# A decoder layer on one core: gate and query projections with the tokens stationary, rotary tables on GpSimd, another opening

## The chip, the cores and the metric

The kernel runs on one core of a Trainium2 chip. A core has five engines that run their own instruction streams and meet through semaphores: TensorE (PE in the profile; its weight loads are PEld), VectorE (DVE), ScalarE (ACT), GpSimd (POOL) and SyncE (SP), which here issues every DMA. The metric is the device time of one execution in microseconds. The kernel before takes 640.01 us (median of three runs, 639.51 to 640.58).

## The reference, cut to what matters

One layer of a hybrid decoder: 256 tokens, width 1024, everything in float32.

```python
xn = rmsnorm(h, norm_mix_g)                                  # per token: x * rsqrt(mean(x^2)+EPS) * g
q_a, k_a, v_a, q_b, f_b, i_b, og_b, g_a, g_b = split_cols(xn @ w_in)   # nine projections of 1024 columns
y_a = moba_attention(q_a, k_a, v_a, positions) @ w_br_attn   # 16 heads of 64, rotary on q and k
y_b = hgrn2(q_b, f_b, i_b, og_b, lb, hgrn_norm_g) @ w_br_hgrn          # 8 heads of 128
merged = sigmoid(g_a) * y_a + sigmoid(g_b) * y_b
h = h + merged @ w_out
h = h + memory_cross_attention(...)                          # 4 heads of 256, 256 memory tokens
h = h + (silu(gate) * up) @ w_ffn_out                        # hidden width 2816
out = rmsnorm(h, final_norm_g)

# hgrn2, with lb from a softmax over learned logits
q = silu(q_b) * 128 ** -0.5
f = lb + (1 - lb) * sigmoid(f_b)                             # forget gate
k = 1 - f
S_t = diag(f_t) S_{t-1} + k_t i_t^T ;   o_t = S_t^T q_t
o = rmsnorm_per_head(o) * norm_g * silu(og_b)

# rotary: cos and sin of position * 10000^(-2i/64), i = 0..31
```

## The kernel before, in words

**Weights as 103 chunks.** All weight matrices are cut on the host into chunks of 128x2048 (1 MB each), in the order in which TensorE uses them (`plan`, `ORDER`). To keep float32 accuracy each chunk is split on the chip: `prep` issues the DMA into `raw` (two buffers), ScalarE writes `hi`, the value rounded to fp32r, in two pieces of 1024 columns, and `lo = raw - hi` is made by VectorE (576 columns of each piece) and GpSimd (448 columns, `POOL_COLS` is 896 for a chunk). `hi` and `lo` have three buffers each. A product is three matmuls: hi·hi, hi·lo and lo·hi. `nxt` hands the next chunk to TensorE and prepares the one two ahead (`LEAD`).

**Two forms of product.** In the F form (`f_part`, `gemm_f`) a chunk holds 256 columns and all 1024 rows of the weight; the weight is the stationary operand, the 256 tokens move, and the result has features on partitions: 48 matmuls of 128x256 a chunk. In the T form (`t_part`, `gemm_t`) a chunk holds 512 columns and half of the rows; 128 tokens are stationary, 512 weight columns move, and the result has tokens on partitions: 24 matmuls of 128x512 a chunk, and two chunks make one group of 512 columns for the 256 tokens.

**Order of the work.** TensorE's instructions stand in the order in which the Python code records them; those of ScalarE, VectorE, GpSimd and SyncE are put into an order of their own by a scheduler at build time. Once that order is fixed, each engine runs its list strictly in order: an instruction that waits holds back all that stand behind it. A helper, `tick`, is called after each chunk and advances background work (`bg`) by one step, and `later` holds functions that run at the next tick.

The opening (`opening`, `prep(pieces=4)`) brings the input `xT` and the first two chunks in quarters of 256 KB each; the split input is `Xh`, `Xl`. TensorE first runs 18 matmuls on zeros (`warm`). Then come four F chunks of the forget gate (columns 4096 to 5119 of `w_in`, tiles `psg` and `psf`), whose eviction `ev_f` multiplies by the row factors `rows_x`, applies Sigmoid, and makes the gate `fT` and the keys `KS`; then four F chunks of the recurrence's queries (columns 3072 to 4095), whose eviction `ev_q` makes `QQ` and, on GpSimd, `QP`. The norm factor `r_x` comes from squares of `xraw` on ScalarE and VectorE and two small matmuls, and `rows_x` from two transposes of it. The rotary tables `Ct`, `St` (`rope_tables`, 42 small VectorE instructions and two Sin on ScalarE) are made meanwhile.

All that follows is in T form up to the cross attention: values of the recurrence (`Vb`), then values, queries and keys of the attention, output gate, the two merge gates, and so on. The recurrence itself (`hgrn`: 18 blocks of small matmuls, tiles `l`, `lp`, `lv`, with VectorE work between them) runs as background steps between the chunks, beginning behind the last query chunk. Then come cross attention and feed-forward, which the change does not touch.

Of the kernel before, what the change touches and what calls it, by code (L numbers as in the profile page):

```python
# [24 lines left out]
EPS = 1e-6  # L25
NEG = -1e30
LEAD = 2
POOL_COLS = 896
WARM = 18
# [11 lines left out]
def plan():  # L41
    order = []
    for name, base in (("f", 4), ("q", 3)):
        order += [("F", "w_in", base * 1024 + c * 256) for c in range(4)]
# [4 lines left out]
    for base in (5, 2, 0, 1, 6):  # L49
        order += tgroup("w_in", base * 1024)  # L50
# [61 lines left out]
def build(tc, A, out):  # L112
    nc = tc.nc
    V, SC, G, PE, SY = nc.vector, nc.scalar, nc.gpsimd, nc.tensor, nc.sync
    with ExitStack() as ctx:
# [36 lines left out]
        V.memset(ones, 1.0)  # L152

# [4 lines left out]
        def prep(tags=None, pieces=2, raw=None):  # L158
            i = made[0]
            made[0] += 1  # L160
            if raw is None:
                raw = wr.tile([128, 2048], F32, name="raw", tag="raw")
# [7 lines left out]
            if pieces == 2:  # L170
                SY.dma_start(raw, A["w"][i])
            for c in range(pieces):
                a = slice(c * n, (c + 1) * n)
                if pieces > 2:
                    SY.dma_start(raw[:, a], A["w"][i][:, a])
                    yield
                SC.activation(hi[:, a], raw[:, a], AF.Copy)  # L177
                cut = (c + 1) * n - POOL_COLS // pieces
                for eng, b in ((V, slice(c * n, cut)), (G, slice(cut, (c + 1) * n))):
                    eng.tensor_tensor(lo[:, b], raw[:, b], hi[:, b].bitcast(F32), op=ALU.subtract)  # L180
# [128 lines left out]
        opening = [prep(pieces=4), prep(pieces=4, raw=big("B14", "raw1", (128, 2048)))]  # L309
        for c in range(4):  # L310
            SY.dma_start(xraw[:, 2 * c:2 * c + 2], A["xT"][:, 2 * c:2 * c + 2])
            for g in opening:
                next(g)
            for k in (2 * c, 2 * c + 1):
                g1 = gv[:, V_MIX + k:V_MIX + k + 1]
                if k % 2 == 0:
                    SC.activation(Xh[:, k], xraw[:, k], AF.Copy, scale=g1)
                else:
                    V.tensor_scalar(Xh[:, k], xraw[:, k], g1, None, op0=ALU.mult)
                V.scalar_tensor_tensor(Xl[:, k], xraw[:, k], g1, Xh[:, k].bitcast(F32),  # L320
                                       op0=ALU.mult, op1=ALU.subtract)
        for g in opening:
            run(g)
# [19 lines left out]

        def ev_f(c):
            def ev(ps):
                for m in range(2):
                    h = 2 * c + m
                    t = t2("fraw", (128, 256))
# [760 lines left out]
```

## Time and profile before

| | |
|---|---|
| median of three runs | 640.01 us (639.51 to 640.58) |
| the profiled execution's own time | 641.26 us |
| its span, first to last instruction | 639.5 us |
| mean granted TensorE clock | 0.991 |
| instructions | 9044 |
| first matmul on weights | 7.39 us |
| start of the first `Vb` chunk | 66.98 us |

In the lines of the profile, `L177 ACT ... hi<-raw 128x1024` is a group of instructions of line 177 on ScalarE that write `hi` from `raw`; "x186" is how many, then come busy time in us and the mean of one in ns, and behind the bar the idle time of the engine before them with what ended it. A row of the timeline has start, duration, engine, line, operation and tiles, a count, and in brackets the idle time before it with what ended it. A row of the table by stage gives for a stretch of time the busy time of every engine, the granted TensorE clock as a share of full speed, the DMA engines' busy share and their rate. Matmuls are pipelined: a 128x512 matmul is listed with 390 ns, and the next one starts 227 ns after it. What TensorE needs for a block of work is therefore read from start to start.

### The profile page before, as it was taken

Reading aid. Unit: us, or ns where it says so; the run is one execution under the profiler, and the core shown is the slowest. Engines: PE = TensorE matmul, PEld = TensorE weight load, DVE = VectorE, ACT = ScalarE, POOL = GpSimd, SP = SyncE. Lnnn points to the kernel's source line nnn. Section 1 sums busy time; section 2 is a strip of 40 time slices with the busy share of each in tenths; the row PEclk is TensorE's granted clock in tenths of the full one; section 3 lists DMA queues with packets and bytes.
Section 4 is the critical chain, followed back from the end, with each engine's and each line's share of the span. In section 5 each row is a group of like instructions: output and inputs, shape, how many; then the busy total and the mean of one; then the engine's idle time right before and its main releaser. Section 6 shows DMA issues by size and latency. Waiting matters only on the chain.

```text
span 639.5 us, 9044 instructions
## 1 busy us (share of the span) xinstructions
PE 624.7 (98%) x3428; PEld 533.6 (83%) x3428; DVE 405.9 (63%) x713; ACT 321.5 (50%) x506; POOL 369.4 (58%) x258
## 2 busy tenths in 40 slices
PE   8989999999999999999999999999999999999995
PEld 7979888888887877778889999888888888888884
DVE  6996898789857777695556546764344444444433
ACT  5383564433368666673446445564444444444433
POOL 3468654376554664346766767656565555665552
PEclk9998999999999999999999999999999999999998
DMA  8634554444443333545545455462355554555511
GB/s 282 216 128 162 197 198 169 157 166 138 152 179 132 132 132 132 181 149 197 180 155 192 148 197 183 165 248 81 133 197 198 181 175 178 194 194 197 198 67 66
DMA packets 17036, 107.56 MB, mean 168 GB/s; under 512 B 2144, under 2 KB 2272, under 8 KB 4576
## 3 DMA queue, kind: packets, MB, share of 16 engines
q1 hardware_dynamic: 16992, 106.98, 47.2%
q8 instruction: 27, 0.44, 0.3%
q14 instruction: 17, 0.14, 0.1%
HBM read 105.92 MB, written 1.05 MB: 167 GB/s over the span
## 4 chain that ended last, share of the span: by engine, by line
PE 91%; DVE 3%; POOL 2%; issue 2%; DMA 1%; ACT 1%; SPq 0%; POOLq 0%; DVEq 0%
PE pst L220 13%; PE pst L222 13%; PE pst L221 13%; PE psi L222 6%; PE psi L220 6%; PE psi L221 6%; PE psf L217 3%; PE psf L216 3%; PE psf L215 3%; PE acc L222 3%; PE acc L220 3%; PE acc L221 3%; PE lp L524 2%; PE pso L220 1%; PE pso L222 1%
## 5 line engine op out<-in xcount | busy, mean ns | idle before, releaser
L180 POOL TENSOR_TENSOR lo<-raw,hi 128x448 fp32r<-128x448 f32 (+1 forms) x194 | 298.5, 1554 | 207.9 <-ACT hi L177 198.2
L177 ACT ACTIVATE hi<-raw 128x1024 fp32r<-128x1024 f32 (+1 forms) x194 | 195.6, 1036 | 189.6 <-PE pst L222 79.3
L180 DVE TENSOR_TENSOR lo<-raw,hi 128x576 fp32r<-128x576 f32 (+1 forms) x194 | 197.4, 1021 | 122.5 <-ACT hi L177 121.3
L220 PE MATMUL pst<-hi,Xh 128*128 128x512 f32 x224 | 90.5, 404 | 0.0
L222 PE MATMUL pst<-hi,Xl 128*128 128x512 f32 x224 | 87.4, 390 | 0.0
L221 PE MATMUL pst<-lo,Xh 128*128 128x512 f32 x224 | 87.3, 390 | 0.0
L220 PE MATMUL psi<-hi,h2h 128*128 128x512 f32 x176 | 69.6, 395 | 0.0
L222 PE MATMUL psi<-hi,h2l 128*128 128x512 f32 x176 | 68.6, 390 | 0.0
L221 PE MATMUL psi<-lo,h2h 128*128 128x512 f32 x176 | 68.5, 389 | 0.0
L222 PEld LDWEIGHTS pst<-hi,Xl 128*128 128x128 f32 x224 | 42.0, 188 | 9.0
L220 PEld LDWEIGHTS pst<-hi,Xh 128*128 128x128 f32 x224 | 42.1, 188 | 8.7 <-issue 0.7
L221 PEld LDWEIGHTS pst<-lo,Xh 128*128 128x128 f32 x224 | 42.1, 188 | 7.9
L222 PEld LDWEIGHTS psi<-hi,h2l 128*128 128x128 f32 x176 | 33.0, 188 | 7.1
L221 PEld LDWEIGHTS psi<-lo,h2h 128*128 128x128 f32 x176 | 33.1, 188 | 6.6
L220 PEld LDWEIGHTS psi<-hi,h2h 128*128 128x128 f32 x176 | 33.1, 188 | 6.5
L220 PE MATMUL acc<-hi,hid 128*128 128x512 f32 x88 | 34.3, 390 | 0.0
L222 PE MATMUL acc<-hi,hid 128*128 128x512 f32 x88 | 34.2, 389 | 0.0
L221 PE MATMUL acc<-lo,hid 128*128 128x512 f32 x88 | 34.2, 389 | 0.0
L217 PE MATMUL psf<-Xh,lo 128*128 128x256 f32 x96 | 29.3, 306 | 4.1 <-DVE lo L180 2.2
L215 PE MATMUL psf<-Xh,hi 128*128 128x256 f32 x96 | 28.6, 298 | 0.0
L216 PE MATMUL psf<-Xl,hi 128*128 128x256 f32 x96 | 28.3, 295 | 0.0
L1000 DVE SCALAR_TENSOR_TENSOR fu<-psi,r_h,fg 128x256 f32<-128x256 f32 x22 | 10.6, 484 | 26.0 <-ACT fg L998 25.8
(316 smaller groups left out, 1266.8 us busy)
## 6 DMA issues: line engine op xcount, KB each, us to landing
raw<-w SPq DMA_DIRECT2D x95, 1024.0 KB, 4.8
raw<-w SPq DMA_DIRECT2D x8, 256.0 KB, 5.6
xraw<-xT SPq DMA_DIRECT2D x4, 256.0 KB, 5.5
H<-xtok SPq DMA_DIRECT2D x1, 1024.0 KB, 8.7
mraw<-mT SPq DMA_DIRECT2D x1, 1024.0 KB, 5.6
out<-H SPq DMA_DIRECT2D x4, 256.0 KB, 2.2
gfin<-gfin SPq DMA_DIRECT2D x1, 512.0 KB, 6.5
cst<-cst SPq DMA_DIRECT2D x1, 272.0 KB, 5.7
```

The lines of the kernel that those rows point to most:

```text
L177: SC.activation(hi[:, a], raw[:, a], AF.Copy)
L180: eng.tensor_tensor(lo[:, b], raw[:, b], hi[:, b].bitcast(F32), op=ALU.subtract)
L215: PE.matmul(ps, lh, rh, start=first, stop=False)
L216: PE.matmul(ps, lh, rl, start=False, stop=False)
L217: PE.matmul(ps, ll, rh, start=False, stop=last)
L220: PE.matmul(ps, xh, h, start=first, stop=False)
L221: PE.matmul(ps, xh, l, start=False, stop=False)
L222: PE.matmul(ps, xl, h, start=False, stop=last)
L524: PE.matmul(ps[:, j], KS[:, a0 + j], QQ[:, a0 + j], start=True, stop=True)
L1000: V.scalar_tensor_tensor(u, ps[:, 256:512], r, g, op0=ALU.mult, op1=ALU.mult)
```

## The change

The change touches the opening, the gate and query projections, the rotary tables and a few steps that hang on them:

- The four F chunks of the gate and the four F chunks of the queries become four and four T chunks. The gate's come in the order: columns 0 to 511 rows 0 to 511, columns 512 to 1023 rows 0 to 511, then the other halves of the rows. The evictions work on tokens-on-partitions tiles: Tanh (gate) and Silu (queries) on ScalarE with the per-token factor as scale, straight from PSUM. The results are then turned by TensorE, 8 transposes of 128x128 for each half (`turned`, two ticks later), and `fT`, `KS`, `QP`, `QQ` are made from the turned tiles. `QP` is made on VectorE from PSUM, no longer on GpSimd, and `QQ` is copied by ScalarE.
- `r_x` comes from two ScalarE squares over the token-major input `H` (1024 columns, with an accumulator), so the load of `H` is recorded at the opening; `rows_x`, the squares of `xraw`, two small matmuls and two transposes go.
- The input comes in six transfers instead of four, the first two of 128 KB; the second chunk's quarters come behind all quarters of the first, and the second half of the input behind those.
- For the first eight chunks (`ALONE`) all of `lo` is made by VectorE.
- `rope_tables` runs on GpSimd: each multiply-add becomes two instructions, and an absolute value goes to ScalarE.
- The recurrence starts one tick later, and no drain stands before its output stage. The queries no longer carry a factor of two, hence 128 instead of 512 times EPS.
- A one-element Exp stands at ScalarE's head.

```diff
...
 LEAD = 2
 POOL_COLS = 896
+ALONE = range(8)
 WARM = 18
...
-    for name, base in (("f", 4), ("q", 3)):
-        order += [("F", "w_in", base * 1024 + c * 256) for c in range(4)]
...
+    order += [("T", "w_in", 4096 + c * 512, kh) for kh in range(2) for c in range(2)]
+    for base in (3, 5, 2, 0, 1, 6):
         order += tgroup("w_in", base * 1024)
...
+        warm_act = cp.tile([128, 1], F32, name="warm_act")
+        SC.activation(warm_act, ones, AF.Exp)
...
+            pieces = 4 if first else 2
             n = 2048 // pieces
...
-                cut = (c + 1) * n - POOL_COLS // pieces
+                cut = (c + 1) * n - (0 if i in ALONE else POOL_COLS // pieces)
                 for eng, b in ((V, slice(c * n, cut)), (G, slice(cut, (c + 1) * n))):
-                    eng.tensor_tensor(lo[:, b], raw[:, b], hi[:, b].bitcast(F32), op=ALU.subtract)
+                    if b.start < b.stop:
+                        eng.tensor_tensor(lo[:, b], raw[:, b], hi[:, b].bitcast(F32), op=ALU.subtract)
...
+        opening = [prep(), prep(raw=big("B14", "raw1", (128, 2048)))]
+
...
+        def take_x(a, b):
+            SY.dma_start(xraw[:, a:b], A["xT"][:, a:b])
+
+        for k in range(4):
+            if k in (0, 1, 2):
+                take_x(k, (1, 2, 4)[k])
+            next(opening[0])
+            part_x(k)
+        run(opening[0])
+        run(opening[1])
+        for k in (4, 6):
+            take_x(k, k + 2)
+        for k in range(4, 8):
+            part_x(k)
...
+        gate_a = cp.tile([128, 8], F32, name="gate_a")
+        gate_b = cp.tile([128, 8], F32, name="gate_b")
+        V.tensor_scalar(gate_a, oml, 0.5, None, op0=ALU.mult)
+        V.tensor_tensor(gate_b, lbt, gate_a, op=ALU.add)
...
+        def turned(th, c, use):
+            def turn():
+                for b in range(2):
+                    bk = bank("fT_", (128, 2, 256))
+                    for j in range(2):
+                        for t in range(2):
+                            PE.transpose(bk[:, j, t * 128:(t + 1) * 128],
+                                         th[t][:, (2 * b + j) * 128:(2 * b + j + 1) * 128], ident)
+                    use(4 * c + 2 * b, bk)
+            later.append(lambda: later.append(turn))
...
+            th = {}
+
+            def use(h0, bk):
+                for j in range(2):
+                    h = h0 + j
+                    dst = fT[:, 2 * h:2 * h + 2].rearrange("p a b -> p (a b)")
+                    if j == 0:
+                        SC.activation(dst, bk[:, j], AF.Identity, scale=gate_a[:, h:h + 1], bias=gate_b[:, h:h + 1])
+                    else:
+                        V.tensor_scalar(dst, bk[:, j], gate_a[:, h:h + 1], gate_b[:, h:h + 1],
+                                        op0=ALU.mult, op1=ALU.add)
+                a = slice(2 * h0, 2 * h0 + 4)
+                SC.activation(KS[:, a], fT[:, a], AF.Copy, scale=-1.0, bias=1.0)
+
+            def ev(t, ps):
+                th[t] = t2("fth")
+                SC.activation(th[t], ps, AF.Tanh, scale=r_half[:, t:t + 1])
+                if t == 1:
+                    turned(th, c, use)
...
+            def use(h0, bk):
+                a = slice(2 * h0, 2 * h0 + 4)
+                q4 = bk.rearrange(v4, a=2)
+                V.tensor_tensor(QP[:, a], q4, fT[:, a], op=ALU.mult)
+                SC.activation(QQ[:, a, 64:192], q4, AF.Copy)
                 odd = QP[:, a].rearrange("p a (b c) -> p a b c", c=2)[:, :, :, 1]
                 SC.activation(QQ[:, a, 0:64], odd, AF.Copy)
+
+            def ev(t, ps):
+                th[t] = t2("qth")
+                SC.activation(th[t], ps, AF.Silu, scale=r_x[:, t:t + 1])
+                if t == 1:
+                    turned(th, c, use)
...
-        pss = [[p.tile([128, 256], F32, name="psg", tag=n) for _ in range(2)]
-               for p, n in ((mm, "mm"), (sm, "sm"))]
+        run(prep())
+        run(prep())
         SY.dma_start(cst, A["cst"])
         run(prep())
+        SY.dma_start(H, A["xtok"])
         SY.dma_start(lm, A["lm"])
         SY.dma_start(posi, A["pos"])
...
-        for c in range(4):
-            square(xraw, c)
-        feature_sum(xraw)
-        w2 = by_k(nxt(1), 8)
...
-        r_x = feature_rstd(xraw, "x")
...
-        rows_x = rows_of(r_x, "x", "rowsA")
-        f_part(ps3[:, 1], w3, X, 1, range(7, 8))
-        for c, ps in enumerate(pss + [ps2, ps3]):
-            ev_f(c)(ps)
...
+        for t in range(2):
+            t_part(pss[0][t], w, X, t, 1)
+        ssqx = small("ssqx", [2])
+        junk = big("B9", "junk", (128, 2, 1024))
+        for t in range(2):
+            SC.activation(junk[:, t], H[:, t], AF.Square, accum_out=ssqx[:, t:t + 1])
+        r_x = rstd_of(ssqx, "x")
         r_half = cp.tile([128, 2], F32, name="r_half")
         V.tensor_scalar(r_half, r_x, 0.5, None, op0=ALU.mult)
+        ev = ev_f(0)
+        for t in range(2):
+            ev(t, pss[0][t])
+        tick()
+        w = by_k(nxt(), 4)
+        ev = ev_f(1)
+        for t in range(2):
+            t_part(pss[1][t], w, X, t, 1)
+            ev(t, pss[1][t])
+        tick()
...
-            V.tensor_copy(posf, posi)
...
             def rnd(o, src, c):
-                V.tensor_scalar(o, src, c, None, op0=ALU.mult)
-                V.tensor_scalar(o, o, RND, None, op0=ALU.add)
-                V.tensor_scalar(o, o, RND, None, op0=ALU.subtract)
+                G.tensor_scalar(o, src, c, None, op0=ALU.mult)
...
             def acc(o, a, c, b):
-                V.scalar_tensor_tensor(o, a, float(c), b, op0=ALU.mult, op1=ALU.add)
+                G.tensor_scalar(u, a, float(c), None, op0=ALU.mult)
+                G.tensor_tensor(o, u, b, op=ALU.add)
...
+            G.tensor_tensor(r, r, ml, op=ALU.add)
+            yield 1
+            G.tensor_scalar(r, r, lim, -lim, op0=ALU.min, op1=ALU.max)
+            yield 1
+            SC.activation(t, r, AF.Abs)
+            G.tensor_scalar(t, t, -1.0, TWO_PI / 4, op0=ALU.mult, op1=ALU.add)
+            yield 1
             SC.activation(m, r, AF.Sin)
             SC.activation(mh, t, AF.Sin)
             for i in range(2):
                 rs = r_x[:, i:i + 1]
...
-                    V.tensor_scalar(Ct[:, i, c * 32:(c + 1) * 32], mh[:, i], rs, None, op0=ALU.mult)
...
+                    G.tensor_scalar(Ct[:, i, c * 32:(c + 1) * 32], mh[:, i], rs, None, op0=ALU.mult)
...
-                    V.tensor_scalar(v, ssq, 1.0 / 128.0, 512.0 * EPS, op0=ALU.mult, op1=ALU.add)
+                    V.tensor_scalar(v, ssq, 1.0 / 128.0, 128.0 * EPS, op0=ALU.mult, op1=ALU.add)
...
+        start(rt)
+        for c in range(2):
+            gemm_t(X, ev_q(c))
         hg = hgrn()
-        for c in range(4):
-            if c == 2:
-                start(hg)
-            gemm_f(X, ev_q(c), bank("psf", (128, 2, 256)) if c == 0 else None)
-        start(rt)
+        next(hg)
+        start(hg)
...
-        drain(hg)
...
-        SY.dma_start(H, A["xtok"])
```

In the order that the scheduler gave the changed kernel, ScalarE's list reads, from the gate's last evictions on: the two ScalarE parts of the first turned gate half (`fT`), `hi` of the sixth chunk (two pieces), two `KS`, the absolute value of the rotary chain, a load of the Sin table, the first Sin, `hi` of the seventh chunk (two pieces), two `fT`, the second Sin, a load of the Silu table, the first query eviction, `hi` of the eighth chunk with two `KS` between, the second query eviction. GpSimd's list reads: `r_x`, then the rotary chain, with the six products `Tt` of the recurrence's first four heads among its last steps, then the tables, the other `Tt`, and from the ninth chunk on `lo`. TensorE's list reads: four gate chunks, 8 transposes, the first query chunk, 8 transposes, two query chunks, 8 transposes, the last query chunk, the first `Vb` chunk, 8 transposes, the recurrence's first block, the next `Vb` chunk. SyncE's list reads: input and first two chunks, third and fourth chunk, constants, `H`, fifth chunk, masks, positions, then the rest.

More of the change, by code (lines that the diff above doesn't have):

```diff
@@ L168, in prep @@
                 lo = big(tags[1], "lox", (128, 2048), F32R)
+            pieces = 4 if first else 2
             n = 2048 // pieces
-            if pieces == 2:
+            if not first:
                 SY.dma_start(raw, A["w"][i])
@@ L354, in ev_f @@
             return ev
         def ev_q(c):
[L357 to L366 removed]
+            th = {}
```

100 lines of the change are left out of this document (36 added, 64 removed).

## The prediction

> **What bounds the kernel now.** I read the page's shares first, then TensorE's waits, then the table by stage for the first 66 us.
>
> ```profile
> PE 624.7 (98%) x3428; PEld 533.6 (83%) x3428; DVE 405.9 (63%) x713; ACT 321.5 (50%) x506; POOL 369.4 (58%) x258
> PE 91%; DVE 3%; POOL 2%; issue 2%; DMA 1%; ACT 1%; SPq 0%; POOLq 0%; DVEq 0%
> ```
>
> TensorE is busy 624.7 of 639.5 us and carries 91% of the chain that ended last. What the change can win is TensorE's work, its waits, or its slow clock.
>
> ```profile
> PE psf L217 <- DVE lo L180: 2.2, 3, 0.9
> PE psf L217 <- POOL lo L180: 1.8, 1, 1.8
> PE psg L215 <- ACT hi L177: 1.6, 1, 1.6
> PE warm L308 <- DVE still L305: 1.6, 1, 1.6
> ```
>
> These are all waits of the whole span, and all lie in the gate and query stage: behind it TensorE is never idle.
>
> ```profile
> 0.00:7.40 7.40, 4.22 (x19) 3.92 (x19) 2.85 (x15) 2.67 (x5) 0.20 (x4) 1.00 0.62 161
> 7.40:13.40 6.00, 6.00 (x27) 5.84 (x27) 5.70 (x10) 4.75 (x9) 4.89 (x6) 1.00 1.02 372
> 13.40:21.80 8.40, 8.40 (x72) 8.40 (x72) 8.33 (x13) 4.61 (x7) 4.71 (x5) 1.00 0.84 301
> ...
> 41.00:47.00 6.00, 3.96 (x29) 3.35 (x27) 6.00 (x12) 5.75 (x10) 5.61 (x8) 1.00 0.24 100
> 47.00:53.00 6.00, 4.86 (x22) 4.86 (x23) 2.80 (x4) 0.15 (x1) 5.76 (x8) 0.54 0.53 175
> 53.00:59.00 6.00, 6.00 (x47) 6.00 (x47) 3.48 (x4) 3.84 (x6) 3.81 (x4) 0.89 0.45 178
> ```
>
> The third column from the right is the granted clock, the last the rate of the transfers in GB/s. At 41 to 47 us TensorE is busy 3.96 of 6.00 us, and behind that the clock is 0.54 and 0.89: 6 x 0.46 + 6 x 0.11 = 3.4 us of work lost. A long wait of TensorE costs itself and up to 3.4 us more. From 7.4 to 13.4 us TensorE does 27 matmuls and afterwards 72 in 8.4 us: the opening, too, runs at about half speed.
>
> **The change, part by part.**
>
> ```profile
> 7.39 0.58 PE L215 MATMUL psg<-Xh,hi 128*128 128x256 f32 x1 [1.61 <-ACT hi L177]
> 13.52 0.28 PE L215 MATMUL psg<-Xh,hi 128*128 128x256 f32 x1
> 17.82 0.28 PE L215 MATMUL psg<-Xh,hi 128*128 128x256 f32 x1
> ...
> 66.98 0.53 PE L220 MATMUL pst<-hi,Xh 128*128 128x512 f32 x1
> ...
> 79.36 1.46 PE L478 MATMUL l<-QQ,KS 128*128 128x192 f32 x8
> 80.52 0.53 PE L220 MATMUL pst<-hi,Xh 128*128 128x512 f32 x1
> 86.11 1.46 PE L478 MATMUL l<-QQ,KS 128*128 128x192 f32 x8
> ...
> 140.14 1.03 PE L656 MATMUL rT<-cst,ra 128*128 128x128 f32 x8
> 141.01 1.47 PE L524 MATMUL lp<-QQ,KS 128*128 128x192 f32 x8
> ```
>
> *TensorE's own work.* From 13.52 to 17.82 us lie 36 matmuls of 128x256: 0.119 us each, 5.73 us for an F chunk of 48. A T chunk of 24 takes 80.52 to 86.11 = 5.59 us. Eight chunks: 45.8 becomes 44.7 us, a gain of 1.1. Eight transposes take 140.14 to 141.01 = 0.87 us; 32 are added, 3.5 us, and six tiny instructions go (about 0.5). Net +1.9 us of work. Any gain must come from the waits and the clock.
>
> *Opening.*
>
> ```profile
> 4.83 0.51 ACT L317 ACTIVATE Xh<-xraw,gv 128x256 fp32r<-128x256 f32 x1 [1.65 <-DMA xraw<-xT]
> 6.71 1.30 ACT L177 ACTIVATE hi<-raw 128x512 fp32r<-128x512 f32 x2 [1.37 <-DMA raw<-w]
> ```
>
> The input's first 256 KB are there at 4.83, the first weight quarter at 6.71, and the first matmul stands behind them at 7.39. With 128 KB of input ahead of the quarter instead of 256, and no quarter of the second chunk beside it, I put its landing in the middle, 5.8, and the first matmul 0.9 us earlier: 6.5 us (between 5.5 and 7.4). Each quarter step of a gate chunk is now 6 matmuls of 128x512, 1.4 us at full clock, against 0.7 us for its 256 KB at 372 GB/s and 0.35 more for 128 KB of input in the first chunk: the transfers keep ahead. The clock stays slow for 6 us before; I take 5 us after, which costs 2.4. So TensorE is through four gate chunks at 6.5 + 4 x 5.45 + 2.4 = 30.7 (5.45 where chunk follows chunk, without the first matmul's longer step), through the first 8 transposes at 31.5, the first query chunk 37.1, 8 transposes 38.0, the second query chunk 43.6. There the seventh chunk is due. These times matter only as long as that chunk is ready; what follows says that it is not.
>
> *The rotary chain on GpSimd, and who queues behind it.* ScalarE's list has the absolute value of that chain, a Sin table load and the first Sin ahead of `hi` of the seventh chunk. ScalarE runs its list in order, so this chunk waits for GpSimd's chain, and TensorE for the chunk.
>
> ```profile
> L496 POOL TENSOR_TENSOR Tt<-fT 128x512 f32<-128x512 f32 x2 | 2.2, 1094 | 1.6 <-DVE fT L351 1.6
> L496 POOL TENSOR_TENSOR Tt<-Tt 128x64 f32<-128x64 f32 x2 | 0.6, 294 | 0.2
> L271 POOL TENSOR_TENSOR r_x<-v__359,nhalf 128x2 f32<-128x2 f32 x1 | 0.7, 707 | 4.2 <-DVE v__359 L269 4.2
> 50.77 1.38 POOL L496 TENSOR_TENSOR Tt<-Tt 128x128 f32<-128x128 f32 x4
> 48.05 1.21 POOL L496 TENSOR_TENSOR Tt<-Tt 128x256 f32<-128x256 f32 x1
> 48.04 0.74 DVE L180 TENSOR_TENSOR lo<-raw,hi 128x576 fp32r<-128x576 f32 x1
> L415 DVE TENSOR_SCALAR rt<-rt 128x64 f32<-128x64 f32 x3 | 0.6, 196 | 0.1
> L425 DVE TENSOR_TENSOR rt<-rt 128x64 f32<-128x64 f32 x1 | 0.2, 227 | 0.0
> L177 ACT ACTIVATE hi<-raw 128x1024 fp32r<-128x1024 f32 x186 | 191.0, 1054 | 188.2 <-PE pst L222 79.3 <-PE psi L222 35.5 <-PE acc L222 28.0
> L446 ACT ACT_TABLE_LOAD x1 | 1.3, 1283 | 0.0
> L832 ACT ACTIVATION_READ_ACCUMULATOR hjunk<-H 128x1 f32 x12 | 2.2, 187 | 0.0
> 33.69 0.26 ACT L446 ACTIVATE rt<-rt 128x64 f32<-128x64 f32 x1 [8.00 <-DVE rt L442]
> L361 ACT ACTIVATE qth<-qraw 128x512 f32<-128x512 f32 x4 | 2.5, 628 | 4.2 <-DVE qraw L360 4.2
> L353 ACT ACTIVATE KS<-fT 128x512 f32<-128x512 f32 x4 | 2.5, 624 | 0.4 <-DVE fT L351 0.3
> L279 ACT ACTIVATE rows_x<-rb 128x256 f32<-128x256 f32 x1 | 0.4, 363 | 0.0
> L360 DVE TENSOR_TENSOR qraw<-psf,rows_x 128x512 f32<-128x512 f32 x4 | 2.7, 680 | 4.7 <-PE psf L217 4.7
> ```
>
> The row of 33.69 shows the pattern already before: ScalarE sat 8.00 us behind VectorE's chain, and `hi` of a chunk stood behind it. The other rows are prices: two evictions and a `KS` (512 columns), a 256-column copy out of PSUM for `fT`, a product out of PSUM on VectorE. Now the new chain's end:
>
> 1. *Start.* `r_x` stands first on GpSimd and needs `H`, which lands behind 6.6 MB. By the table: 7.4 x 161 GB/s = 1.2 MB, 6 x 372 = 2.2, the other 3.2 at 372 to 301 take 8.7 to 10.7: 22.1 to 24.1, I take 23.1. Two squares at 1.05 + 0.19 = 2.5, `r_x` 0.71, a small VectorE step and handovers 0.4: 26.7 us. The fifth chunk, whose buffer is free when the third chunk's `lo` is done (near 20), the masks and the positions (1.3 MB, 3.5 us) are behind `H` on the queue and land by about then, so neither holds the chain up by itself.
> 2. *Length.* 43 instructions stand before the absolute value: 15 with two tensors and 28 with one. The nearest GpSimd row is the two-tensor 128x64 product, 0.294; VectorE takes 0.227 for such a one and 0.196 for a one-tensor one, so I scale: 0.294 x 0.196 / 0.227 = 0.25. Four dependent products take 1.38 us, some 0.08 between two. 15 x 0.37 + 28 x 0.33 = 14.8 us. The six `Tt` between add 1.09 + about 0.65 + 1.38 = 3.1.
> 3. *The shared port.* The 128x256 product at 48.05 took 1.21 us, where 0.65 fits between its neighbours: a VectorE `lo` ran from 48.04 to 48.78. Four `lo` pieces of 1024 columns (576 take 0.74, so 1.3 each) fall into the chain: 3.5 us (between 0 and 5.2).
>
> The chain ends at 26.7 + 14.8 + 3.1 + 3.5 = 48.1 us (bounds: VectorE's 0.196 for the one-tensor ones and no port loss, 43.0; 0.39 for them, twice VectorE, and full loss, 53.7). Then absolute value 0.26, table 1.28, Sin 0.26, first half of `hi` 1.05, its `lo` 1.3: 52.2, less one matmul that needs `hi` alone: 51.9. TensorE waits 51.9 - 43.6 = 8.3 us. The clock falls; of up to 3.4 us I take 2.5.
>
> *The rest of the stage.* Seventh chunk 51.9 + 5.45 + 2.5 = 59.9; transposes 60.7; eighth chunk 66.3. The transposes need both query evictions, which stand far down ScalarE's list: from 49.9 (first Sin done) two `hi` 2.1, two `fT` 0.7, Sin 0.26, table 1.28, eviction 0.63, `hi` 1.05, two `KS` 1.25, `hi` 1.05, eviction 0.63 make 58.9, so they add nothing; had the clock stayed up, they would be the next to be late, by 1.5 us. The first `Vb` chunk thus starts at 66.3 instead of 66.98, but 8 transposes (0.87) and the recurrence's first block (79.36 to 80.52, 1.16), done by then before, still follow: 66.3 + 2.0 = 68.3, that is +1.4 us.
>
> *At nothing.* `lo` on VectorE alone: 2.6 us a chunk against TensorE's 5.6; without that cover the chunk would be late by its excess. The one-element Exp: ScalarE loads a table at the head in both. Table loads before `Vb`: three in both. `H` on SyncE's list stands after two chunks and ahead of the fifth, due at 31.5, which lands near 26. `QP` moves to VectorE (four at 0.68 us), 2.7 us against the two multiplications per eviction that VectorE loses (0.68 and more, four times); it is one of the things that VectorE has room for while TensorE is late. The later tick and the missing drain: 18 blocks fit into the 20 ticks before the output stage.
>
> **Sum:** 640.0 + 1.4 = 641.4 us; against the profiled execution 641.3 + 1.4 = 642.7. The measurement tells about 0.2%, 1.3 us, from no change.
>
> A rule that speaks against this change: the Trainium skill, GPSIMD Engine Reference, section "Performance versus the Vector engine", calls ordinary elementwise work on GpSimd about twice VectorE's time. The rows here show 294 against 227 ns at this size, 1.3 times. By the page's factor on every instruction the chain would be some 6 us longer, an estimate, and the time about 648.
>
> **The rivals.**
>
> *Faster: the chain is shorter than I price it.* GpSimd's one-tensor instructions as short as VectorE's and no loss at the port: end at 43.0, 5.1 us earlier, 641.4 - 5.1 = 636.3. If the chain did not stand in front of the seventh chunk at all, that chunk would start at 43.6 and all follow 8.3 + 2.5 us (wait and clock) earlier: 630.6. It decides from a chain under 18.7 us (I take 21.4), where 1.3 us more are won. For it: TensorE's four waits and the slow clock of before are gone. Against it: the port rows.
>
> *Slower: one-tensor instructions on GpSimd cost twice VectorE's.* 28 x (0.39 + 0.08 - 0.33) = +3.9 us: 645.3. It decides at a chain over 21.3 us, so nearly at once. Against it: 1.3 times for two tensors. [...]
>
> *Slower: a new wait behind the stage.* The recurrence's blocks are TensorE instructions among the chunks: one whose queries or keys are not ready holds all chunks behind it. VectorE is busy 6.00 of 6.00 at 41 to 47 us; should the recurrence's blocks, one tick later, be late once by 1 us, the clock adds up to 3.4: 644 to 646.
>
> *It does nothing:* would need the seventh chunk to be hidden and its gain given back; that is the middle of the first rival, counted there and in the sum's range.
>
> **How the numbers follow.** The sum: 0.44, own range 638.8 to 644 (0.2 within 0.2%, 0.24 slower). Shorter chain: 0.33, all faster. Twice VectorE: 0.15. Late wait: 0.08. Together faster 0.33, same 0.20, slower 0.47. The range 632.5 to 645.8 leaves out the best of the first rival and the worst of the last two.
>
> **What would show it.** Right: the wait of ScalarE for GpSimd's `rt` some 12 us long, ending near 48; one wait of TensorE of 6 to 10 us for `lo` near 44 to 52, a clock of about 0.5 behind it; no TensorE wait later. Wrong: that wait under 3 us (first rival), one-tensor rows on GpSimd of 0.39 us (second), waits behind 70 us (third), or a first matmul later than 7.4 us.

## The result and the profile after

The changed kernel takes 645.7 us (median; 644.65 to 646.84) where the kernel before, on the same chip, takes 640.3 us (639.51 to 640.77): ratio 1.0086, 95% interval 1.0064 to 1.0108. The forecast was 641.4 us. Slower was right as a direction; the size was 0.2% and came out at 0.9%. The profiled execution took 645.16 us, with a span of 643.4.

The page's shares and the shares of the chain that ended last, of the kernel after:

```profile
PE 620.6 (96%) x3262; PEld 521.8 (81%) x3262; DVE 385.2 (60%) x653; ACT 326.2 (51%) x511; POOL 361.4 (56%) x286
PE 90%; POOL 3%; DMA 2%; issue 1%; DVE 1%; ACT 1%; SPq 0%; POOLq 0%; ACTq 0%
```

TensorE is busy 4.1 us less than before in a span 3.9 us longer: it stands still for 8 us more (busy time also counts what a slow clock stretches). Where, the waits of TensorE say (engine, tile and line that waited, what ended the wait; then us in total, times, longest), and the table by stage for the same stretches as before:

```profile
PE pst L225 <- ACT hi L181: 11.7, 1, 11.7
PE warm L313 <- DVE still L310: 1.6, 1, 1.6
PE psg L434 <- DVE lo L185: 1.1, 1, 1.1
PE pst L226 <- DVE lo L185: 0.6, 1, 0.6
```

```profile
0.00:7.40 7.40, 5.26 (x22) 4.53 (x22) 2.82 (x16) 2.84 (x5) 0.19 (x4) 1.00 0.61 161
7.40:13.40 6.00, 5.30 (x23) 4.32 (x24) 6.00 (x13) 5.21 (x9) 0.00 (x0) 1.00 1.03 372
41.00:47.00 6.00, 1.57 (x7) 0.95 (x6) 0.00 (x0) 0.00 (x0) 5.41 (x15) 0.94 0.00 0
47.00:53.00 6.00, 0.00 (x0) 0.00 (x0) 0.00 (x0) 1.52 (x2) 4.02 (x14) 0.50 0.01 3
53.00:59.00 6.00, 4.12 (x9) 2.94 (x10) 3.40 (x4) 5.96 (x10) 3.90 (x9) 0.50 0.17 40
```

The waits for `lo` of the kernel before are gone but for 1.1, 0.6 and 0.3 us, and one wait of 11.7 us has come. From 47 to 53 us TensorE and VectorE do nothing, and the transfers next to nothing; GpSimd works, ScalarE only in the last 1.5 us, and the granted clock falls to 0.50. The timelines of ScalarE and TensorE name the chain behind it:

```profile
33.33 1.15 ACT L390 ACTIVATE KS<-fT 128x512 f32<-128x512 f32 x2
51.46 0.26 ACT L499 ACTIVATE rt<-rt 128x64 f32<-128x64 f32 x1 [16.98 <-POOL rt L497]
51.73 1.28 ACT L502 ACT_TABLE_LOAD   x1
53.02 0.26 ACT L502 ACTIVATE rt<-rt 128x64 f32<-128x64 f32 x1
53.19 1.99 ACT L181 ACTIVATE hi<-raw 128x1024 fp32r<-128x1024 f32 x2
```

```profile
54.28 0.79 PE L225 MATMUL pst<-hi,Xh 128*128 128x512 f32 x1 [11.71 <-ACT hi L181]
55.67 0.79 PE L226 MATMUL pst<-lo,Xh 128*128 128x512 f32 x1 [0.60 <-DVE lo L185]
62.99 0.60 PE L372 MATMUL fT__521<-cst,qth 128*128 128x128 f32 x4
69.31 0.39 PE L225 MATMUL pst<-hi,Xh 128*128 128x512 f32 x1
```

ScalarE is done with `KS` at 34.5, then waits 16.98 us for GpSimd's rotary chain (the absolute value, L499), loads the Sin table, does the first Sin, and only then splits the seventh chunk. TensorE, ready for that chunk since about 42.6, gets it at 54.28 and runs its first half at half clock. The rows of 62.99 and 69.31 are the transposes behind the seventh chunk and the first matmul of the first `Vb` chunk.

GpSimd's and VectorE's rows in that stretch, and two groups of GpSimd:

```profile
27.36 0.18 POOL L462 CAST posf<-posi 128x2 f32<-128x2 int32 x1 [1.86 <-DMA posi<-pos]
27.64 2.81 POOL L466 TENSOR_SCALAR rt<-cst,posf 128x32 f32<-128x32 f32 x2
32.83 1.16 POOL L471 TENSOR_SCALAR rt<-rt 128x64 f32<-128x64 f32 x1
34.07 1.09 POOL L479 TENSOR_SCALAR rt<-rt 128x64 f32<-128x64 f32 x1
51.19 0.24 POOL L497 TENSOR_SCALAR rt<-rt 128x64 f32<-128x64 f32 x1
```

```profile
27.60 2.36 DVE L185 TENSOR_TENSOR lo<-raw,hi 128x1024 fp32r<-128x1024 f32 x2 [1.90 <-ACT hi L181]
32.52 2.40 DVE L185 TENSOR_TENSOR lo<-raw,hi 128x1024 fp32r<-128x1024 f32 x2 [0.40 <-ACT hi L181]
```

```profile
L474 POOL TENSOR_SCALAR rt<-rt 128x64 f32<-128x64 f32 x12 | 4.4, 368 | 0.9
L475 POOL TENSOR_TENSOR rt<-rt 128x64 f32<-128x64 f32 x12 | 3.8, 319 | 0.8
```

The chain begins at 27.36, when the positions land, and ends at 51.43. A one-tensor instruction of 128x64 takes 368 ns on GpSimd, more than a two-tensor one with 319, and 1.9 times VectorE's 196. The stretched rows (1.16 and 1.09 instead of 0.37; 2.81 for a pair that takes 0.72 alone) lie under VectorE's `lo` of 27.60 and 32.52, and nowhere else in the chain.

### The profile page after: what moved, and what is told of

It is laid out like the page before. It is cut to its first block, busy times and chain, and to the rows that moved or that the text cites. A ratio compares the mean times of both kernels' runs of the same rounds, so it can differ in the third digit from the quotient of the medians.

```text
span 643.4 us, 8659 instructions
## 1 busy us (share of the span) xinstructions
PE 620.6 (96%) x3262; PEld 521.8 (81%) x3262; DVE 385.2 (60%) x653; ACT 326.2 (51%) x511; POOL 361.4 (56%) x286
## 4 chain that ended last, share of the span: by engine, by line
PE 90%; POOL 3%; DMA 2%; issue 1%; DVE 1%; ACT 1%; SPq 0%; POOLq 0%; ACTq 0%
PE pst L225 13%; PE pst L226 13%; PE pst L227 13%; PE psi L225 6%; PE psi L227 6%; PE psi L226 6%; PE acc L227 3%; PE acc L225 3%; PE acc L226 3%; PE psf L220 2%; PE psf L221 2%; PE psf L222 2%; PE lp L580 2%; DMA H<-xtok 2%; PE pso L225 1%
## 5 line engine op out<-in xcount | busy, mean ns | idle before, releaser
L185 POOL TENSOR_TENSOR lo<-raw,hi 128x448 fp32r<-128x448 f32 x174 | 275.2, 1595 | 198.5 <-ACT hi L181 195.5
L181 ACT ACTIVATE hi<-raw 128x1024 fp32r<-128x1024 f32 (+1 forms) x194 | 196.3, 1037 | 188.3 <-PE pst L227 66.3
L185 DVE TENSOR_TENSOR lo<-raw,hi 128x576 fp32r<-128x576 f32 (+2 forms) x194 | 196.8, 1020 | 144.9 <-ACT hi L181 143.7
L225 PE MATMUL pst<-hi,Xh 128*128 128x512 f32 x256 | 104.2, 407 | 11.7 <-ACT hi L181 11.7
L226 PE MATMUL pst<-lo,Xh 128*128 128x512 f32 x256 | 100.8, 394 | 0.6 <-DVE lo L185 0.6
L227 PE MATMUL pst<-hi,Xl 128*128 128x512 f32 x256 | 100.6, 393 | 0.0
L225 PEld LDWEIGHTS pst<-hi,Xh 128*128 128x128 f32 x256 | 48.6, 190 | 22.2 <-ACT hi L181 12.1
L226 PEld LDWEIGHTS pst<-lo,Xh 128*128 128x128 f32 x256 | 48.7, 190 | 10.3 <-DVE lo L185 1.1
L227 PEld LDWEIGHTS pst<-hi,Xl 128*128 128x128 f32 x256 | 48.6, 190 | 10.3
L1052 ACT ACTIVATE fg<-psi,r_h 128x256 f32<-128x256 f32 x22 | 10.4, 475 | 29.9 <-PE psi L227 29.9
L227 PEld LDWEIGHTS acc<-hi,hid 128*128 128x128 f32 x88 | 16.5, 188 | 3.4
L225 PEld LDWEIGHTS acc<-hi,hid 128*128 128x128 f32 x88 | 16.5, 188 | 3.4
```

Source lines behind the costliest of these rows:

```text
L225: PE.matmul(ps, xh, h, start=first, stop=False)
L226: PE.matmul(ps, xh, l, start=False, stop=False)
L227: PE.matmul(ps, xl, h, start=False, stop=last)
L1052: SC.activation(g, ps[:, 0:256], AF.Silu, scale=r)
```

## The experiments

Each kernel is compared with the kernel before on the same chip (639.62 to 639.68 us). The changed kernel's 645.7 us stands beside 640.3, so differences between it and the experiments carry some 0.7 us of their own. Theory A all along: the chain costs only through what stands behind it in a list that an engine runs in order. The rivals say that the cost is the clock, the port, or GpSimd's speed as such.

**The rotary tables back on VectorE.** `rope_tables` as in the kernel before, all else as changed; the Sines then stand behind `hi` of the seventh chunk.

```diff
-            G.tensor_copy(posf, posi)
+            V.tensor_copy(posf, posi)
...
-                G.tensor_scalar(u, a, float(c), None, op0=ALU.mult)
-                G.tensor_tensor(o, u, b, op=ALU.add)
+                V.scalar_tensor_tensor(o, a, float(c), b, op0=ALU.mult, op1=ALU.add)
...
```

> The changed kernel, with the rotary tables back on VectorE as in the kernel before (42 instructions, multiply-add as one); the scheduler now puts the Sin behind hi of the seventh chunk and ahead of the eighth chunk's second successor. Theory A: VectorE sat idle for 19 us in that stretch, so the chain costs little there: no long wait of ScalarE, 630 to 634 us. Rival C (the chain is long wherever it runs, and VectorE has all of lo beside it): lo late, several TensorE waits, 636 to 644 us.

Measured: 631.43 us (630.98 to 631.64), ratio 0.9867 [0.9854, 0.9880]. Its waits of TensorE:

```profile
PE warm L313 <- DVE still L310: 1.6, 1, 1.6
PE psg L226 <- DVE lo L185: 0.8, 1, 0.8
PE psg L431 <- ACT hi L181: 0.4, 1, 0.4
```

This one part is worth 14.3 us, and it turns a gain of 8.2 into a loss.

**A shorter chain.** Six of the multiply-adds, 12 GpSimd instructions, leave the chain; the angle is then reduced less finely.

```diff
-            for a, c in ((t, C1), (ml, D2), (mh, D3), (t, C2), (ml, D3), (t, C3), (m, D4)):
+            for a, c in ((t, C1),):
```

> The changed kernel without six of the seven multiply-adds of the last reduction in the rotary angle (12 GpSimd instructions; the angle is then reduced less exactly). Place and order on ScalarE stay. Theory A gives a slope of one: 12 instructions at 0.43 us and five of the six Tt behind the chain (1.8 us) end it 6.9 us earlier, near 44.5 us, TensorE waits about 5 us instead of 11.7, and the time is 645.7 - 6.9 = 638.8 (637 to 640.5). Rival B: less than 3 us won.

Measured: 638.72 us (638.14 to 639.56), ratio 0.9984 [0.9975, 0.9992]. ScalarE's wait for `rt` falls from 16.98 to 10.2 us, the chain ends at 45.15 instead of 51.43, and TensorE's wait is 4.9 instead of 11.7. So 6.3 us less of chain are 7.0 us less of time by the medians and 5.7 by the two profiled executions (645.16 and 639.45): a slope of about one. In this range the chain's end sets the time of the whole kernel.

**The absolute value and the Sines later.** They get a bias of zero made from the last query tile, so that ScalarE's list has them behind the query stage; GpSimd's chain stays.

```diff
-            SC.activation(t, r, AF.Abs)
+            SC.activation(hold, QQ[:, 15, 64:65], AF.Copy, scale=0.0)
+            SC.activation(t, r, AF.Abs, bias=hold)
...
-            SC.activation(m, r, AF.Sin)
-            SC.activation(mh, t, AF.Sin)
+            SC.activation(m, r, AF.Sin, bias=hold)
+            SC.activation(mh, t, AF.Sin, bias=hold)
```

> The changed kernel, with one edit: ScalarE's three rotary instructions (absolute value and two Sin) get a bias of zero that is read from the last turned query, so that they stand behind the query stage in ScalarE's list, and the Sin table is loaded no more on its own. GpSimd's chain is untouched. Theory A (the changed kernel loses its time because the seventh chunk's hi stands behind the chain): TensorE's one wait of 11.7 us and the half clock behind it (some 2.7 us) go, 645.7 - 11.7 - 0.6 - 2.7 = 630.7 us, between 629 and 633; no TensorE wait over 1 us behind the opening. Rival B (the turned evictions on ScalarE, or the transfers, make the seventh and eighth chunk late anyway): a wait of 3 us or more stays near 42 to 60 us, 635 to 642 us.

Measured: 638.58 us (637.31 to 641.1), ratio 0.9986 [0.9975, 0.9997]; a gain of 7 us, not the 15 that I expected. The wait for the seventh chunk is gone, but another has come, in TensorE's timeline and in GpSimd's:

```profile
60.06 0.80 PE L226 MATMUL pst<-lo,Xh 128*128 128x512 f32 x1 [5.04 <-POOL lo L185]
```

```profile
55.53 0.24 POOL L498 TENSOR_SCALAR rt<-rt 128x64 f32<-128x64 f32 x1
55.74 1.04 POOL L554 TENSOR_TENSOR Tt<-fT 128x512 f32<-128x512 f32 x1
56.85 2.07 POOL L554 TENSOR_TENSOR Tt<-Tt 128x256 f32<-128x256 f32 x5
58.88 4.42 POOL L185 TENSOR_TENSOR lo<-raw,hi 128x448 fp32r<-128x448 f32 x4
```

From the ninth chunk on GpSimd makes its share of `lo` again, and this share stands behind the chain and six `Tt` in GpSimd's own list. Rival B's number came true (635 to 642 us, a wait of over 3 us), but not its reason: what ended the wait is neither a turned eviction nor a transfer. I had looked at one list only.

**The same, and `lo` of the ninth and tenth chunk on VectorE alone.** This tells the second queue from the port: the chain is there in full, but nothing due stands behind it.

```diff
-ALONE = range(8)
+ALONE = range(10)
```

> The kernel with the late absolute value and Sines still waited 5.0 us for GpSimd's share of `lo` of the ninth chunk, at 60.06 us, with 6.8 us of half clock behind it (58.2 to 65.1): that `lo` stands in GpSimd's own list behind the whole rotary chain, which ended at 55.8. Here `lo` of the ninth and tenth chunk is also made by VectorE alone; nothing else differs from that kernel. Theory A (the chain costs nothing by itself, only through what stands behind it in an ordered list, first ScalarE's, then GpSimd's): no TensorE wait over 1 us behind the first 20 us, no half clock in the stage, 638.6 - 5.0 - 2.5 to 3.4 = 630.2 to 631.1 us, as with the tables on VectorE (631.4). Rival B (GpSimd's chain also slows VectorE's `lo` at the port they share, and the stage is late by that): a wait for VectorE's `lo` takes its place, 633 to 638.

Measured: 630.91 us (630.37 to 631.07), ratio 0.9859 [0.9846, 0.9872]. The waits of TensorE:

```profile
PE psg L431 <- ACT hi L181: 1.8, 2, 1.1
PE warm L313 <- DVE still L310: 1.6, 1, 1.6
PE fT__353 L372 <- ACT fth L394: 0.4, 1, 0.4
PE psg L226 <- DVE lo L185: 0.3, 1, 0.3
```

No wait is left behind 31 us, although the chain here is longer than in the changed kernel: it begins at 28.8 and ends at 61.4. The same GpSimd work in the same two-instruction form costs nothing measurable against the tables on VectorE (the intervals overlap; what two more chunks of `lo` on VectorE win by themselves was not run). Rival B falls: the place was the cost, on two lists one behind the other. This is the fastest kernel of the study, 8.8 us under the kernel before and 14.8 under the changed one.

**The clock kept up.** 100 matmuls on data at hand, whose result nobody reads, stand ahead of the second query group.

```diff
-        for c in range(2):
-            gemm_t(X, ev_q(c))
+        gemm_t(X, ev_q(0))
+        warm2 = bank("warm2", (128, 256))
+        for _ in range(100):
+            PE.matmul(warm2, Xh[:, 0, :128], Xh[:, 0], start=True, stop=True)
+        gemm_t(X, ev_q(1))
```

> The changed kernel with 100 additional matmuls of 128x256 (11.9 us at full clock), whose result nobody reads, ahead of the seventh chunk, where TensorE waits 11.7 us. It prices the clock alone. If the half clock behind the wait costs TensorE some 2.7 us: 643.0 us (642 to 644). If the stretch behind it is bound by ScalarE's list anyway: 645 to 646.5. If the clock counted nothing and the extra matmuls delayed the chunk: over 646.5.

Measured: 645.26 us (644.0 to 646.02), ratio 1.0080 [1.0067, 1.0093], which can't be told from the changed kernel's 1.0086. The stage behind the chain, by the table:

```profile
47.00:53.00 6.00, 6.00 (x53) 6.00 (x52) 0.00 (x0) 0.26 (x1) 4.97 (x16) 1.00 0.01 4
53.00:59.00 6.00, 4.83 (x30) 3.97 (x29) 3.40 (x4) 5.94 (x9) 2.89 (x9) 1.00 0.00 0
```

The clock is 1.00 where it was 0.50, and nearly nothing is won. Two things eat it: the positions landed later in this execution (the chain began at 28.26 instead of 27.36, and ScalarE's wait ended at 52.74, 1.28 us later), and the transposes then wait for the query eviction (`PE fT__622 <- ACT qth`, 0.5 us), which ScalarE reaches at 62.35. With the chain at its old end that eviction would be done 1.3 us before 62.99, so no more than 1.3 of the 2.5 us that I had put down for the clock could have been had. Whether the positions land late in the other executions too is not shown, so this run does not price the clock by itself.

**`lo` shared again, tables on VectorE.** The first experiment's kernel with `ALONE = range(0)`.

```diff
-ALONE = range(8)
+ALONE = range(0)
```

> The changed kernel with the rotary tables on VectorE (631.4) and, besides, `lo` of the first eight chunks shared again between VectorE and GpSimd as before: the price of the step that gives these eight to VectorE. Theory A (that step only frees GpSimd for the rotary chain and is worth little by itself, since VectorE has room): 631 to 632.5. Rival B (a piece of `lo` that GpSimd shares is ready later, 448 columns in some 1.6 us on GpSimd against 1024 in 1.25 on VectorE, and the stage waits for it as the kernel before did, 1.8 us once and 2.2 in three, with the clock behind it): 633 to 637.

Measured: 634.34 us (633.95 to 636.5), ratio 0.9925 [0.9909, 0.9942]. Giving `lo` to VectorE alone is thus worth 2.9 us even where the rest of the change stands. Rival B's amount is right, but its waits stayed short (1.1 us in the longest line); the reason is below.

**One part alone: `lo` on VectorE alone, in the kernel before.**

```diff
+ALONE = range(8)
...
-                cut = (c + 1) * n - POOL_COLS // pieces
+                cut = (c + 1) * n - (0 if i in ALONE else POOL_COLS // pieces)
```

> The kernel before with another part alone: `lo` of the first eight chunks by VectorE alone. Nothing else differs. Theory A (VectorE is the engine that the gate and query stage of the kernel before waits for, busy 47.4 of its first 60 us and all of 41 to 47; 448 of every 1024 columns more on it, some 0.5 us a piece and 8 us in all, make it later): 642 to 648, with TensorE waits for VectorE's `lo`, and none for GpSimd's. Rival B (the pieces on GpSimd, 1.6 us each, are what is late, 1.8 us in one wait): 636 to 639.

Measured: 632.87 us (632.63 to 633.07), ratio 0.9892 [0.9877, 0.9908]. My theory had it slower by 2 to 8 us; it is faster by 6.8, more than Rival B's 1 to 4 as well, and no wait is left but 2.1 us for VectorE's `lo` and small ones. Behind 47 us the clock is now 1.00, where the kernel before had 0.54 and 0.89 behind its waits for `lo`:

```profile
47.00:53.00 6.00, 6.00 (x53) 6.00 (x52) 4.06 (x7) 4.55 (x6) 1.39 (x2) 1.00 0.39 162
53.00:59.00 6.00, 6.00 (x48) 5.92 (x47) 5.74 (x6) 2.67 (x4) 4.54 (x3) 1.00 0.48 175
```

In these 12 us TensorE does 101 matmuls instead of 69, 3.8 us of work at 0.12 us each, of the 8.6 us between the two profiled executions (632.63 and 641.26). VectorE's and GpSimd's groups in the first 60 us, of the kernel before, and VectorE's of this kernel:

```profile
L180 DVE TENSOR_TENSOR lo<-raw,hi 128x576 fp32r<-128x576 f32 x12 | 12.4, 1043 | 0.5 <-ACT hi L177 0.5
L180 DVE TENSOR_TENSOR lo<-raw,hi 128x288 fp32r<-128x288 f32 x8 | 5.8, 744 | 0.7 <-ACT hi L177 0.7
...
L180 POOL TENSOR_TENSOR lo<-raw,hi 128x448 fp32r<-128x448 f32 x12 | 17.5, 1481 | 6.6 <-ACT hi L177 6.6
L180 POOL TENSOR_TENSOR lo<-raw,hi 128x224 fp32r<-128x224 f32 x8 | 6.6, 840 | 11.2 <-DMA raw<-w 7.0 <-ACT hi L177 4.2
```

```profile
L182 DVE TENSOR_TENSOR lo<-raw,hi 128x1024 fp32r<-128x1024 f32 x12 | 15.1, 1295 | 1.4 <-ACT hi L178 1.4
L182 DVE TENSOR_TENSOR lo<-raw,hi 128x512 fp32r<-128x512 f32 x8 | 5.3, 685 | 0.1
```

In the opening VectorE needs 744 ns for 288 columns beside GpSimd, and 685 ns for 512 columns alone. All 20 pieces cost it 18.2 us shared (12.4 + 5.8) and 20.4 us alone (15.1 + 5.3): it takes over 78% more columns for 2.2 us, not 8, and GpSimd's 24.1 us go. Where a VectorE `lo` of 288 columns overlaps no instruction of GpSimd (14.27 and 14.64 us in the kernel before) it takes 446 ns. The two engines wait for each other. The Trainium skill, SBUF — State Buffer, section "Who interferes with whom", has the rule: VectorE with two inputs in SBUF contends with a GpSimd instruction that reads SBUF, and which of the two blocks is decided by who came first. These rows bear it out in both directions: here VectorE is stretched, and in the changed kernel GpSimd's short steps are (2.81, 1.16, 1.09), while VectorE's `lo` pieces, which began first, take 2.36 and 2.40 us a pair beside them, against 2.35 in the kernel with `lo` on VectorE alone.

**One part alone: the tables on GpSimd, in the kernel before** (`rope_tables` as in the change), and **both parts** together with `ALONE`.

```diff
-            V.tensor_copy(posf, posi)
+            G.tensor_copy(posf, posi)
...
-                V.scalar_tensor_tensor(o, a, float(c), b, op0=ALU.mult, op1=ALU.add)
+                G.tensor_scalar(u, a, float(c), None, op0=ALU.mult)
+                G.tensor_tensor(o, u, b, op=ALU.add)
...
```

> The kernel before with one part of the change alone: the rotary tables on GpSimd, in their two-instruction form, with the absolute value on ScalarE. The order that results has the absolute value, the Sin table load and both Sines ahead of `hi` of the fifth chunk on ScalarE, and pieces of `lo` among the chain's steps on GpSimd. Theory A (what counts is what stands behind the chain in an ordered list): in the kernel before the chain on VectorE ended at 33.7 and `hi` of the fifth chunk began at 33.85; on GpSimd the chain of some 20 us, four pieces of `lo` at 1.6 us and stretches at the port, begun at 15 to 22, end it between 44 and 52. The fifth chunk, due at about 30, is late by 10 to 17 us more than before, and the clock falls behind that: 650 to 660. Rival B (the chain leaves VectorE, which is busy 6.00 of 6.00 us at 41 to 47, and that relief pays for the later Sines): 636 to 642.

> The kernel before with both parts: the rotary tables on GpSimd and `lo` of the first eight chunks on VectorE; gate and queries stay in F form, the opening is that of before. In the order that results GpSimd has nothing ahead of the chain, which begins when the positions are there, and the absolute value and the Sines stand behind the first query eviction on ScalarE, not ahead of a gate chunk. Theory A (place in the lists): the chain of some 21 us and its stretches end near 40, before ScalarE comes to it, so it costs nothing; VectorE gives up some 10 us of chain and takes 8 us of `lo`: 636 to 641, far from the 645.7 of the whole change. Rival B (the chain on GpSimd is slow by itself, wherever it stands): 644 to 650.

Measured: 652.32 us (652.08 to 652.35), ratio 1.0195 [1.0181, 1.0208] for the tables alone, and 642.98 us (642.62 to 643.77), ratio 1.0051 [1.0038, 1.0063] for both. Waits of ScalarE and TensorE of the first, then of the second:

```profile
ACT rt L445 <- POOL rt L443: 19.9, 1, 19.9
...
PE psf L217 <- DVE lo L180: 6.7, 5, 4.6
PE psf L217 <- POOL lo L180: 3.7, 3, 1.3
PE psf L215 <- ACT hi L177: 3.3, 1, 3.3
```

```profile
ACT rt L447 <- POOL rt L445: 6.7, 1, 6.7
ACT rt L451 <- POOL rt L448: 4.7, 1, 4.7
...
PE psf L217 <- ACT hi L178: 7.8, 1, 7.8
```

The first came out as Theory A has it, though the chain ended at 43.5, a little ahead of the 44 to 52. For the second my number was wrong by 2 us and more: I had the chain end near 40, it ended at 49.4, because `r_x` stands among its first steps in GpSimd's list and held it up for 4.2 us, and because the one-tensor price holds here too; ScalarE's absolute value and Sines stand behind it, with a chunk's `hi` behind them. The second wait of 4.7 us is GpSimd's list again: the step between the absolute value and the second Sin, at 55.65, stands behind twelve `Tt`. So the move costs 12.7 us in the kernel before, 10.1 there with `lo` on VectorE (642.98 against 632.87), 14.3 in the changed kernel, and nothing where nothing due queues behind it.

**The opening's break.** The kernel before with 25 matmuls on zeros at the head instead of 18.

```diff
-WARM = 18
+WARM = 25
```

> The kernel before, with 25 matmuls on zeros at the head instead of 18, so that they end near 7.2 us, where the first matmul on weights starts at 7.39, instead of 5.8. No work on weights changes. Theory A (the break of 1.6 us between the zeros and the weights is what kept the TensorE clock at half until 13.4 us, and the changed kernel has full clock from 5.3 us because its weights follow the zeros without a break): the matmuls of 128x256 from 7.4 us on step by 0.12 us instead of 0.21, up to 6.0 x 0.5 = 3.0 us less, but the transfers of the opening may then bind: 636.6 to 638.5. Rival B (the clock rises at a fixed time or with what the transfers bring): unchanged, 639.5 to 640.3. Rival C (the transfers bind the opening anyway): full clock but unchanged time.

Measured: 639.71 us (639.42 to 640.63), ratio 0.9998 [0.9990, 1.0007]. Its table by stage:

```profile
7.40:13.40 6.00, 5.72 (x45) 5.52 (x46) 5.21 (x11) 4.24 (x8) 4.09 (x5) 1.00 1.03 368
13.40:21.80 8.40, 7.08 (x55) 6.47 (x54) 8.29 (x15) 5.07 (x8) 4.06 (x5) 1.00 0.90 323
```

TensorE does 45 matmuls from 7.4 to 13.4 us instead of 27, and 55 from 13.4 to 21.8 instead of 72: what it wins it waits out again for `lo`, with VectorE busy 8.29 of 8.40 us. That is rival C, except that VectorE binds and not the transfers. By 47 us both have done the same 266 matmuls behind those on zeros, and the medians agree: the slow opening cost the kernel before nothing that can be measured. The two profiled executions (639.42 and 641.26 us) differ only later, where the clock from 47 to 53 us is 0.72 instead of 0.54; why is not shown.

Theory A's cause is not shown either. With 18 matmuls on zeros, the tables-alone kernel has a break of 1.11 us and steps of 0.12 us from 7.6 us on, and the kernel with both parts a break of 0.18 us and steps of 0.21 until 10.5 us. The granted clock, too, reads 1.00 in all of these stretches, so that the half pace is the clock is read from the steps alone.

## Why the prediction was right or wrong

**TensorE's own work: too dear by about 1 us.** No run isolates it. In the kernel with the tables on VectorE the first query chunk takes 5.55 us from start to start, the next two 10.98, and eight transposes 0.79. With 5.5 for all eight chunks (an estimate: the gate's chunks are taken like the queries') that is 44.0 + 3.2 us against 45.8, less 0.5 for the tiny instructions: +0.9 where I had +1.9. All that the change does besides `lo` and the tables, this work included, is worth 5.3 us with `lo` shared (634.34 against 639.68) and 1.4 beyond `lo` on VectorE alone (631.43 against 632.87).

**Opening: too careful.** The first matmul came at 5.76, not 6.5, and the next ones step at 0.23 us, the full pace, so that the 2.4 us for a slow start were not paid. Against this stood waits for `lo` that I had not counted (1.1 and 0.3 us). The second query chunk was over at about 42.6, not 43.6. It changed nothing, as the step itself said, since the seventh chunk was not there.

**The chain in front of the seventh chunk: the mechanism right, the size off, and this is the step that failed.** "*Length.*" priced the one-tensor GpSimd instruction at 0.25 us by scaling with VectorE's ratio (0.196 to 0.227). On GpSimd that ratio is turned round: 0.368 against 0.319. Term by term, from the timeline: start 27.36 instead of 26.7 (the positions, not `r_x`, came last: the step had them "land by about then"); 28 one-tensor instructions with their gaps 12.0 us without the port, instead of 9.2; 15 two-tensor ones 5.7 instead of 5.55; six `Tt` 2.8 instead of 3.1; the port 3.6 instead of 3.5 (2.11 + 0.78 + 0.72 in the stretched rows). Together 24.1 us instead of 21.4, an end at 51.4 instead of 48.1. The 3.3 us go through nearly undiminished: the seventh chunk was done at 62.99 instead of 59.9, the first `Vb` chunk began at 69.31 instead of 66.3. The rival "one-tensor instructions cost twice VectorE's" named this price (0.39) and gave 645.3 us. It had 0.15. The row against it was a two-tensor one, and said nothing about the other form. The Trainium skill, GPSIMD Engine Reference, section "Engine selection", has one-input work "roughly line-rate" on GpSimd; these rows, with 1.9 times VectorE for one input and 1.4 for two, say otherwise at 128x64. That section gives its factor of two for two inputs; the prediction's 648 us laid a factor of two on every instruction.

**A second term: the reference time.** By starts the change costs 69.31 + 2.0 - 66.98 = 4.3 us, and the two profiled executions differ by 3.9 (645.16 - 641.26), but the medians by 5.4. The profiled execution of before was 1.25 us above its median. I read a start from that execution and added the difference to the median. With 25 matmuls on zeros, a kernel of the same median, the first `Vb` chunk began at 65.15 us in an execution of 639.42: the later start of 66.98 belongs to the longer execution. This puts the sum 1.25 us low, and with the 3.0 us at the first `Vb` chunk (69.31 against 66.3) it makes up the miss of 4.3.

**The clock: the 2.5 us were there and cost less.** The first 11 matmuls of the seventh chunk, from 54.28 to 60.03 us, took 5.15 us without the wait among them, where 11 x 0.227 = 2.5 are due: 2.65 us. But keeping the clock up moved the median by 0.4 us, less than its interval. In its profiled execution the chain ended 1.28 us later, and ScalarE's list set the next step. The prediction had this ("they would be the next to be late, by 1.5 us") and still took the clock off in full for the case that "the chain did not stand in front of the seventh chunk at all"; there it belongs, and 630.6 stands against 630.91 and 631.43. That they are so close is partly luck: the opening (1.0 us too late) and the reference time (1.25 us too low) were both off there, in opposite directions.

**`lo` on VectorE alone, put under "At nothing": wrong.** It hardly touched the number, since the sum goes by starts and has no waits for `lo` ahead of the seventh chunk; as an account of what the change wins it is wrong. It is worth 6.8 us in the kernel before and 2.9 in the changed one. I had counted VectorE's columns and not the two engines' waiting for each other, though the row of 48.05 used for the chain shows the same port.

**Rest.** No TensorE wait came behind 60 us, so "a new wait behind the stage" fell in the changed kernel; it came true as soon as the first wait was taken away (60.06, on GpSimd's list).

## What to carry to other kernels

Moving work to an idle engine is priced by what stands behind it in every ordered list it passes, not by that engine's load: the same chain cost 14 us, 7 us or nothing depending on whether a chunk's `hi` (ScalarE) or `lo` (GpSimd) queued behind it. Look through all lists before moving, because the second wait shows only when the first is gone. And take a price only from a row of the same form on the same engine: where there is none, let both ends carry chances, not the scaled middle.

## What the hardware showed that I had not expected

- On GpSimd a 128x64 instruction with one tensor input takes 368 ns, one with two inputs 319 ns; on VectorE it is 196 and 227.
- Sharing `lo` slows VectorE: it took 744 ns for 288 columns beside GpSimd, 446 where the two did not overlap, and 685 ns for 512 columns without GpSimd.
- The one that comes second is stretched: VectorE's `lo`, begun at 27.60 us, took 2.36 us a pair beside the chain, as without it, and GpSimd's 128x32 step, begun at 27.64, took 2.47 us instead of 0.36.
